# Between two stages of a hybrid decoder layer: the order of the second half's first products, and of a norm's sums

## Chip, cores and metric

The kernel runs on one core of a Trainium2 chip. The metric is the device time of the whole program in microseconds (us), the median of three runs.

## What is computed

One decoder layer on 512 tokens of width 1024, in float32: a gated feed-forward sub-layer, a mixing sub-layer (attention beside a state-space model), and a second feed-forward sub-layer. A norm stands before and behind each of them. Cut to what matters here:

```python
def rms_norm(x, g):
    y = x * lax.rsqrt(jnp.mean(x * x, axis=-1, keepdims=True) + NORM_EPS)
    return y * g

h = rms_norm(x, ffn1_pre_g)
x = x + 0.5 * rms_norm(swiglu(h, ffn1_w_in, ffn1_w_out), ffn1_post_g)
h = rms_norm(x, mix_pre_g)
proj = h @ w_mix_in                 # q, k, v, u
...                                 # attention and state-space model
x = x + rms_norm(mixed, mix_post_g)
h = rms_norm(x, ffn2_pre_g)
x = x + 0.5 * rms_norm(swiglu(h, ffn2_w_in, ffn2_w_out), ffn2_post_g)
```

The place of the change is between two sub-layers: from the last products of one, through its post-norm, the residual sum and the next pre-norm, to the first products of the next.

## The kernel before

Activations lie transposed: 8 k-tiles (`KD`) of 128 channels by 512 tokens. Each float32 product is made of three (`mm3`): an operand is rounded to a high part (`whi`, `xh`), the rest is its low part (`wlo`, `xl`), and high x high, high x low and low x high are added up in one PSUM bank. The high part is a cast on ScalarE (L93 for weights, L143 for activations), the low part a subtract on VectorE or GpSimd (L95, L144).

`boundary` stands between two stages and is called twice: between the first feed-forward stage and the mixing stage, and between that and the second feed-forward stage. Tokens are taken there in two halves of 256 (`h` 0 and 1). In order:

- The last products of the old stage (`product`, tile `yt`), first half and then second half, their sums into `y` (`gather`, L286) and the squares of `y` (`squares`).
- For each half the post-norm (`post[h]`): `sums` adds the squares over the channels with tiny products against ones (tile `st`), VectorE scales the result (`nv`, L182), GpSimd raises it to the power -1/2 (L184); `spread` copies the result to all partitions with four products (tile `rp`).
- `prep(h, k)` makes k-tile k of the next stage's input: VectorE scales `y` (L301), adds it to the residual `x` (L303), ScalarE makes `xh`, VectorE `xl`; ScalarE squares the new `x` and GpSimd adds the square to the next norm's sum (`sq_acc`, L155).
- `begin(h, k)` multiplies k-tile k with four chunks of the next stage's weights (`w`), three products each, into four banks (`first`). It is done on `x` before its norm; the norm's factor is applied to the results later.
- `pre[0]` is the next pre-norm's factor for the first half, `pre[1]` for the second; `pre[1]` is handed on and done inside the next stage.

In the second half, k-tiles 0 to 3 are multiplied k-tile by k-tile. Then come the sums of `pre[0]`, and then chunk by chunk: chunk 0 with k-tiles 4 to 7, chunk 1 with k-tiles 4 to 7, the spreading of `pre[0]`, and chunks 2 and 3. The post-norm of the second half, `post[1]`, is done inside the first half's products: its sums behind k-tile 3, its spreading behind k-tile 5.

The next stage begins with its own weight chunks (`prj` in the mixing stage, `gu` in the feed-forward stage). Rounded weights have four buffers for the high part and four for the low part (`wtiles`), and the four chunks of `boundary` fill all of them; raw weights have three.

Matmuls keep the order in which they are written. Most instructions of the other engines are put in order by the compiler's planner, which goes by its own estimate of what is ready; an instruction marked `fix` is pinned behind the one that was written just before it on its engine.

Of the kernel before, what the change touches and what calls it, by code (L numbers as in the profile page):

```python
# [20 lines left out]
KD = D // P  # L21
# [19 lines left out]
class Layer:  # L41
# [70 lines left out]
    def fix(self, i):  # L112
        return self.tc.keep_in_program_order(i)
# [143 lines left out]
    def boundary(self, y, tail, ipost, half, inext, chunks):  # L257


        nc = self.nc  # L260
        w = [self.load(c, (KD, P), pool=i % 2 == 1) for i, c in enumerate(chunks)]
        tw = [t.rearrange("p (m k j) -> p m k j", k=NT, j=P) for t in self.tw]
        hs = [slice(0, HT), slice(HT, S)]
        xh, xl = self.ktiles("xh", F32R), self.ktiles("xl", F32R)
        acc2 = self.acct()
        n4, nr = self.rtiles()
        o = [self.bank("first") for _ in w]
        p4 = self.sp.tile([P, 4], F32, name="p4", tag="p4")
        bank, acc = [None], [self.acct(), self.acct()]
        post = [self.rstd(acc[h], p4, None, 2 * h, 2 * h + 2, True) for h in range(2)]  # L270
        rr = [None, None]
        pre = [self.rstd(acc2, n4, nr, 0, 2), self.rstd(acc2, n4, nr, 2, 4)]

        def product(h, m):
            if m % 2 == 0 or m == 7:
                bank[0] = self.bank("yt").rearrange("p (m t) -> p m t", m=2)
            b = bank[0][:, m % 2 if m < 6 else 0]
            for k in range(NT):
                th, tl = tail(k)
                self.mm3(b, tw[0][:, m, k], tw[1][:, m, k], th[:, hs[h]], tl[:, hs[h]], k == 0, k == NT - 1)  # L280
            return bank[0]

        def gather(h, m, n, b, fix=lambda i: i):

            ym = y.pair(slice(m, m + n))[:, :, hs[h]]
            fix(nc.vector.tensor_tensor(out=ym, in0=b[:, :n], in1=ym, op=ALU.add))  # L286

        def squares(h, m, n, eng, fix=lambda i: i):

            m2 = slice(m % 2, m % 2 + n)  # L290
            t = (acc[h] if m == 0 else self.tmp("sq")).rearrange("p (m t) -> p m t", m=2)[:, m2]
            fix(nc.scalar.activation(out=t, in_=y.pair(slice(m, m + n))[:, :, hs[h]], func=AF.Square))
            if m and eng:
                ac = acc[h].rearrange("p (m t) -> p m t", m=2)[:, m2]
                (fix if eng is V else fx)(eng.tensor_tensor(out=ac, in0=ac, in1=t, op=ALU.add))
            return t.rearrange("p m t -> p (m t)")

        def prep(h, k, fix=lambda i: i):
            t = y(k)[:, hs[h]]
            xk = self.x(k)[:, hs[h]]  # L300
            fix(nc.vector.scalar_tensor_tensor(out=t, in0=t, scalar=self.g(ipost, k, half), in1=rr[h],  # L301
                                               op0=ALU.mult, op1=ALU.mult))
            fix(nc.vector.tensor_tensor(out=xk, in0=t, in1=xk, op=ALU.add))  # L303
            self.split(xh(k)[:, hs[h]], xl(k)[:, hs[h]], xk, self.g(inext, k), fix)
            self.sq_acc(acc2[:, hs[h]], xk, k == 0, nc.gpsimd)

        def begin(h, k, only=None):
            for i in range(len(w)) if only is None else (only,):
                self.mm3(o[i][:, hs[h]], w[i][0][:, k], w[i][1][:, k], xh(k)[:, hs[h]], xl(k)[:, hs[h]],
                         k == 0, k == KD - 1)  # L310

        V, G, fx = nc.vector, nc.gpsimd, self.fix
        b2 = [self.bank("yt")[:, :HT] for _ in range(2)]
        for ks in (range(NT - 1), (NT - 1,)):
            for m in range(2):
                for k in ks:
                    th, tl = tail(k)
                    self.mm3(b2[m], tw[0][:, m, k], tw[1][:, m, k], th[:, hs[0]], tl[:, hs[0]], k == 0, k == NT - 1)
        for m in range(2):
            gather(0, m, 1, b2[m].unsqueeze(1))  # L320
        squares(0, 0, 2, V)
        for m in range(2, KD):
            b = product(0, m)
            if m % 2 or m > 5:
                m, n = (m - 1, 2) if m < 6 else (m, 1)
                gather(0, m, n, b)
                squares(0, m, n, G if m == 2 else V)
        late = []
        for m in range(KD):
            b = product(1, m)  # L330
            if m % 2 or m > 5:
                m1, n = (m - 1, 2) if m < 6 else (m, 1)
                gather(1, m1, n, b)
                t = squares(1, m1, n, G if n == 2 else None)
                if n == 1:
                    late.append(t)
                if m == 5:
                    self.fold(acc[1], G, fx)
            if m == 2:
                post[0][0](fixp=fx)  # L340
            if m == 3:
                rr[0] = post[0][1]()
                for k in range(2):
                    prep(0, k)
        for k in range(KD):
            if k > 1:
                prep(0, k, fx if k > 5 else lambda i: i)
            begin(0, k)
            if k == 3:
                post[1][0](late, fix=fx)  # L350
            if k == 5:
                rr[1] = post[1][1]()
        for k in range(4):
            prep(1, k)
            begin(1, k)
        pre[0][0](fixp=fx)
        for k in range(4, KD):
            prep(1, k)
        for i in range(len(w)):
            for k in range(4, KD):  # L360
                begin(1, k, i)
            if i == 1:
                pre[0][1]()
        self.xh, self.xl = xh, xl
        return o, n4, nr, pre[1]
# [827 lines left out]
```

## Time and profile before

| | us |
|---|---|
| three runs | 978.39, 980.96, 981.84 |
| median | 980.96 |
| profiled execution, its own time | 978.9 |
| its span | 977.1 |

The profile is one execution, and its times count from the start of its span. PE is TensorE's matmul, PEld its weight load, DVE VectorE, ACT ScalarE, POOL GpSimd. A row of the timeline gives the start, the duration, the engine, the line, the operation, what it writes and reads, and how many instructions were merged; in brackets stands how long the engine was idle just before, and what it waited for. Most of TensorE's instructions have L121, a helper's line, so they are told apart by their tiles. `ymix` is `y` in the second call.

### The profile page before, as it was taken

The page shows a single profiled execution, that of the slowest core. Times are in us where ns is not written, and L with a number is a line of the kernel's source. Part 1 is how long each engine was busy: PE and PEld are TensorE (multiplying, and loading weights), DVE is VectorE, ACT ScalarE, POOL GpSimd, SP SyncE. Part 2 cuts the span into 40 slices and gives each one's busy share as a digit, 9 for nine tenths or more (in the row PEclk, how much of TensorE's full clock was granted, in tenths as well). Part 3 has the DMA queues.
Part 4 walks back from the last instruction along what each step waited for, and adds up shares of the span by engine and source line. Part 5 has one row for each costly group of instructions (what it writes and reads, how often), then busy time and mean ns, then how long its engine had stood idle before and what let it go on. Part 6 is the DMA issues. An engine that isn't in the chain of part 4 may idle for free.

```text
span 977.1 us, 12902 instructions
## 1 busy us (share of the span) xinstructions
PE 948.4 (97%) x5088; PEld 792.6 (81%) x5088; DVE 532.9 (55%) x938; ACT 372.3 (38%) x616; POOL 223.5 (23%) x134
## 2 busy tenths in 40 slices
PE   9999999999999999999999699999999999999996
PEld 7888888888888899878667589888888888888884
DVE  7997214553265447658769567564225433444426
ACT  7353334431233234356553654443333222323312
POOL 2322212322233134300000024422122212222300
PEclk9999999999999999999999999999999999999998
DMA  8223334343343230473111530222223222333202
GB/s 261 91 103 113 103 119 150 100 166 103 108 131 116 76 130 23 118 211 120 54 51 50 185 126 23 92 95 93 89 87 108 101 93 87 108 98 131 95 0 87
DMA packets 38606, 102.48 MB, mean 105 GB/s; under 512 B 7665, under 2 KB 10737, under 8 KB 38001
## 3 DMA queue, kind: packets, MB, share of 16 engines
q1 hardware_dynamic: 37680, 98.50, 31.6%
q10 hardware_dynamic: 864, 3.15, 0.9%
q8 instruction: 40, 0.66, 0.3%
q14 instruction: 22, 0.17, 0.1%
HBM read 94.03 MB, written 7.60 MB: 104 GB/s over the span
## 4 chain that ended last, share of the span: by engine, by line
PE 86%; DVE 7%; ACT 3%; DMA 2%; issue 1%; POOL 0%; DVEq 0%; POOLq 0%; ACTq 0%
PE gu L121 46%; PE yo L121 20%; PE prj L121 6%; PE yt L121 5%; PE first L121 4%; PE st L121 1%; DVE sx L1064 1%; DVE Hs L1064 1%; DVE xl L144 1%; DMA wraw<-wmot 1%; DVE x L303 1%; PE pt L820 1%; ACT sc L795 1%; DMA w<-w2d 1%; PE idle L121 1%
## 5 line engine op out<-in xcount | busy, mean ns | idle before, releaser
L93 ACT CAST whi<-wraw 128x1024 fp32r<-128x1024 f32 (+5 forms) x161 | 155.8, 971 | 323.8 <-PE gu L121 126.9
L95 POOL TENSOR_TENSOR wlo<-wraw,whi 128x1024 fp32r<-128x1024 f32 (+2 forms) x62 | 156.3, 2521 | 525.9 <-ACT whi L93 525.9
L121 PE MATMUL gu<-xh,whi 128*128 128x512 f32 x656 | 257.6, 393 | 0.0
L121 PE MATMUL gu<-xh,wlo 128*128 128x512 f32 x656 | 255.6, 390 | 0.0
L121 PE MATMUL gu<-xl,whi 128*128 128x512 f32 x656 | 255.3, 389 | 0.0
L95 DVE TENSOR_TENSOR wlo<-wraw,whi 128x1024 fp32r<-128x1024 f32 (+5 forms) x99 | 111.6, 1130 | 124.9 <-ACT whi L93 124.5
L121 PEld LDWEIGHTS gu<-xh,wlo 128*128 128x128 f32 x656 | 123.1, 188 | 25.9
L121 PEld LDWEIGHTS gu<-xl,whi 128*128 128x128 f32 x656 | 123.2, 188 | 25.1
L121 PEld LDWEIGHTS gu<-xh,whi 128*128 128x128 f32 x656 | 123.2, 188 | 25.1 <-issue 0.4
L405 DVE TENSOR_TENSOR ut<-gu,rs 128x512 f32<-128x512 f32 x41 | 28.3, 689 | 104.0 <-PE gu L121 103.8
L141 DVE TENSOR_TENSOR al<-ut,ah 128x512 fp32r<-128x512 f32 x44 | 69.0, 1570 | 24.9 <-ACT ah L140 24.8
L121 PE MATMUL yo<-ah,whi 128*128 128x512 f32 x144 | 56.0, 389 | 0.0
L121 PE MATMUL yo<-al,whi 128*128 128x512 f32 x144 | 56.0, 389 | 0.0
L121 PE MATMUL yo<-ah,wlo 128*128 128x512 f32 x144 | 56.0, 389 | 0.0
L121 PE MATMUL yo<-whi,ah 128*128 128x512 f32 x144 | 56.0, 389 | 0.0
L121 PE MATMUL yo<-wlo,ah 128*128 128x512 f32 x144 | 56.0, 389 | 0.0
L121 PE MATMUL yo<-whi,al 128*128 128x512 f32 x144 | 56.0, 389 | 0.0
L403 DVE TENSOR_TENSOR gt<-gu,rs 128x512 f32<-128x512 f32 x41 | 28.2, 688 | 50.7 <-PE gu L121 50.6
L140 ACT CAST ah<-ut 128x512 fp32r<-128x512 f32 x44 | 27.2, 621 | 58.3 <-DVE ut L406 58.2
L121 PE MATMUL first<-xl,whi 128*128 128x256 f32 (+1 forms) x144 | 43.3, 300 | 2.2 <-DVE xl L144 2.2
L121 PE MATMUL first<-xh,whi 128*128 128x256 f32 (+1 forms) x144 | 43.9, 305 | 0.9 <-ACT xh L143 0.9
L406 DVE TENSOR_TENSOR ut<-ut,gt 128x512 f32<-128x512 f32 x44 | 40.7, 927 | 3.7
(192 smaller groups left out, 1426.9 us busy)
## 6 DMA issues: line engine op xcount, KB each, us to landing
wraw<-w2i SPq DMA_DIRECT2D x44, 512.0 KB, 3.5
wraw<-w1i SPq DMA_DIRECT2D x42, 512.0 KB, 3.5
wraw<-w2o SPq DMA_DIRECT2D x18, 512.0 KB, 3.5
wraw<-wmi SPq DMA_DIRECT2D x16, 512.0 KB, 3.5
wraw<-w1o SPq DMA_DIRECT2D x16, 448.0 KB, 3.4
x<-xT SPq DMA_DIRECT2D x8, 256.0 KB, 4.5
w1d<-w1s SPq DMA_DIRECT2D x8, 256.0 KB, 2.9
w2d<-zb SPq DMA_DIRECT2D x2, 1024.0 KB, 4.9
```

The source lines that it names most:

```text
L93: fix(self.nc.scalar.copy(out=hi, in_=raw))
L95: fix(eng.tensor_tensor(out=lo, in0=raw, in1=hi.bitcast(F32), op=ALU.subtract))
L121: i = self.nc.tensor.matmul(*a, **k)
L140: nc.scalar.copy(out=hi, in_=src)
L141: nc.vector.tensor_tensor(out=lo, in0=src, in1=hi.bitcast(F32), op=ALU.subtract)
L144: fix(nc.vector.scalar_tensor_tensor(out=lo, in0=src, scalar=scale, in1=hi.bitcast(F32), op0=ALU.mult, op1=ALU.subtract))
L303: fix(nc.vector.tensor_tensor(out=xk, in0=t, in1=xk, op=ALU.add))
L403: nc.vector.tensor_tensor(out=gt, in0=o[f][0], in1=r, op=ALU.mult)
L405: nc.vector.tensor_tensor(out=ut, in0=o[f][1], in1=r, op=ALU.mult)
L406: nc.vector.tensor_tensor(out=ut, in0=ut, in1=gt, op=ALU.mult)
L795: nc.scalar.activation(out=so, in_=so, func=AF.Exp, bias=nm[:, t:t + 1], scale=-1.0, accum_out=den[:, t:t + 1])
L1064: tt = lambda o, x, y, op: self.fix(V.tensor_tensor(out=o, in0=x, in1=y, op=op))
```

## The change

The second half's products go k-tile by k-tile to the end; the sums of `pre[0]` stay behind k-tile 3, and its spreading stands behind k-tile 6. The sums of `post[1]` stand behind the first half's k-tile 2 instead of 3, and its spreading behind k-tile 4 instead of 5.

```diff
-        def begin(h, k, only=None):
-            for i in range(len(w)) if only is None else (only,):
+        def begin(h, k):
+            for i in range(len(w)):
                 self.mm3(o[i][:, hs[h]], w[i][0][:, k], w[i][1][:, k], xh(k)[:, hs[h]], xl(k)[:, hs[h]],
                          k == 0, k == KD - 1)
...
             if k > 1:
                 prep(0, k, fx if k > 5 else lambda i: i)
             begin(0, k)
-            if k == 3:
+            if k == 2:
                 post[1][0](late, fix=fx)
-            if k == 5:
+            if k == 4:
                 rr[1] = post[1][1]()
-        for k in range(4):
+        for k in range(KD):
             prep(1, k)
             begin(1, k)
-        pre[0][0](fixp=fx)
-        for k in range(4, KD):
-            prep(1, k)
-        for i in range(len(w)):
-            for k in range(4, KD):
-                begin(1, k, i)
-            if i == 1:
+            if k == 3:
+                pre[0][0](fixp=fx)
+            if k == 6:
                 pre[0][1]()
```

## Rows read from the trace of the kernel before

**Rows 1.** The page's part 4: the chain that ended last, by engine.

```profile
PE 86%; DVE 7%; ACT 3%; DMA 2%; issue 1%; POOL 0%; DVEq 0%; POOLq 0%; ACTq 0%
```

**Rows 2.** The chain in order of time, 605 to 626: start, us, what.

```profile
619.21 0.99 DVE xl L144
...
622.18 0.44 PE rp L121 x4
```

**Rows 3.** The timeline of TensorE in the second call, 603 to 640.

```profile
603.13 1.03 PE L121 MATMUL st<-ones,sq 128*128 128x2 f32 x8
...
606.98 0.60 PE L121 MATMUL rp<-ident,p 128*128 128x128 f32 x4
...
610.18 0.28 PE L121 MATMUL first<-xh,wlo 128*128 128x256 f32 x1
610.30 0.28 PE L121 MATMUL first<-xh,whi 128*128 128x256 f32 x1
610.90 0.38 PE L121 MATMUL first<-xl,whi 128*128 128x256 f32 x1 [0.32 <-DVE xl L144]
...
616.63 0.50 PE L121 MATMUL st<-ones,acc 128*128 128x2 f32 x4
...
620.24 0.38 PE L121 MATMUL first<-xl,whi 128*128 128x256 f32 x1 [0.63 <-DVE xl L144]
...
621.78 0.28 PE L121 MATMUL first<-xl,whi 128*128 128x256 f32 x1
...
625.34 0.40 PE L121 MATMUL gu<-xh,whi 128*128 128x512 f32 x1
...
626.04 0.40 PE L121 MATMUL gu<-xh,whi 128*128 128x512 f32 x1
...
633.30 0.61 PE L121 MATMUL rp<-ident,r 128*128 128x128 f32 x4
```

**Rows 4.** The timeline of VectorE, second call, 603 to 627.

```profile
603.26 0.42 DVE L303 TENSOR_TENSOR x<-ymix,x 128x256 f32<-128x256 f32 x1
...
605.51 0.15 DVE L182 TENSOR_SCALAR nv<-st 128x2 f32<-128x2 f32 x1
606.17 0.48 DVE L144 SCALAR_TENSOR_TENSOR xl<-x,sm,xh 128x256 fp32r<-128x256 f32 x1 [0.51 <-ACT xh L143]
607.62 0.87 DVE L301 SCALAR_TENSOR_TENSOR ymix<-ymix,sm,rp 128x256 f32<-128x256 f32 x2 [0.96 <-PE rp L121]
608.41 1.65 DVE L303 TENSOR_TENSOR x<-ymix,x 128x256 f32<-128x256 f32 x2
...
610.37 0.47 DVE L144 SCALAR_TENSOR_TENSOR xl<-x,sm,xh 128x256 fp32r<-128x256 f32 x1
...
621.75 1.74 DVE L95 TENSOR_TENSOR wlo<-wraw,whi 128x1024 fp32r<-128x1024 f32 x1 [1.56 <-ACT whi L93]
```

**Rows 5.** The timeline of GpSimd, second call, 603 to 640.

```profile
605.75 0.71 POOL L184 TENSOR_TENSOR p<-nv,mhalf 128x2 f32<-128x2 f32 x1 [3.59 <-DVE nv L182]
606.42 3.35 POOL L155 TENSOR_TENSOR acc<-acc,sq 128x256 f32<-128x256 f32 x4
...
619.18 3.23 POOL L155 TENSOR_TENSOR acc<-acc,sq 128x256 f32<-128x256 f32 x4
...
628.07 2.38 POOL L95 TENSOR_TENSOR wlo<-wraw,whi 128x1024 fp32r<-128x1024 f32 x1 [2.31 <-ACT whi L93]
```

**Rows 6.** The timeline of ScalarE, second call, 603 to 640.

```profile
620.66 1.05 ACT L93 CAST whi<-wraw 128x1024 fp32r<-128x1024 f32 x1 [1.18 <-PE first L121]
622.10 1.05 ACT L93 CAST whi<-wraw 128x1024 fp32r<-128x1024 f32 x1 [0.38 <-PE first L121]
...
626.94 1.05 ACT L93 CAST whi<-wraw 128x1024 fp32r<-128x1024 f32 x1 [1.91 <-DMA wraw<-w2i]
```

**Rows 7.** All instructions that write `wlo`: ns min/median/max, first and last start.

```profile
L95 DVE TENSOR_TENSOR wlo<-wraw,whi x99: 284/1224/2584, 6.8 to 919.6; 128x1024 fp32r<-128x1024 f32 x72, 128x512 fp32r<-128x512 f32 x12, 128x896 fp32r<-128x896 f32 x8, 128x256 fp32r<-128x256 f32 x4
```

**Rows 8.** The timeline of TensorE in the first call, 388 to 407.

```profile
390.33 0.28 PE L121 MATMUL first<-xh,whi 128*128 128x256 f32 x1
...
405.38 0.40 PE L121 MATMUL prj<-xh,whi 128*128 128x512 f32 x1
...
406.08 0.40 PE L121 MATMUL prj<-xh,whi 128*128 128x512 f32 x1
```

## The prediction, made before the changed kernel was run

> **What bounds the kernel now.** I read the page first, for the chain that ended last: TensorE carries 86% of it [rows 1]. Time is won only where TensorE waits, or where something that TensorE waits for comes earlier. Then I read the timeline of TensorE through the two calls of `boundary`. Both look alike: the first product of the second token half starts at 390.33 in the first call and at 610.30 in the second, and the next stage's first product starts 15.05 and 15.04 us later [rows 3, 8]. I work with the second call and carry the result to the first.
>
> In the second half TensorE starts a product every 0.12 us (610.18, 610.30) [rows 3]. Its 96 products would take 11.52 us. The next norm's sums (616.63) and their spreading interrupt them once each; the chain gives 0.44 us for the spreading [rows 2], and I take the same for the sums. So the half needs 12.40 us and takes 15.04: **2.64 us are waits**, with the slower restart after each. There are four waits. The first is at k-tile 0 (0.32 us idle at 610.90, VectorE's `xl` late), the last at k-tile 7 (0.63 us at 620.24, again `xl`) [rows 3]. The chain of waits between them runs through VectorE: its `xl` of k-tile 7 starts at 619.21 and takes 0.99 [rows 2]. The reader is to see why it is wanted so early: after k-tile 3 the kernel takes weight chunk 0 through k-tiles 4 to 7 at once, so k-tile 7 is wanted nine products (1.1 us) after k-tile 4, while VectorE makes k-tiles at the pace of one in some 1.3 us (`xl` of k-tile 0 ends at 610.84, of k-tile 7 at 620.20).
>
> Last I read ScalarE, for what the chunk order buys today. The next stage's weights are rounded into buffers that the four chunks hold. The cast at 622.10 starts 0.04 us after the last product that reads the high part of chunk 1 (starts 621.78, takes 0.28) [rows 3, 6]. The chunk-by-chunk end frees the first chunk early, and the rounding of the next weights hides under the other three.
>
> **The change, part by part.** No instruction is added or removed; the same products and sums are issued in another order, and no transfer is issued among the moved steps.
>
> *K-tile by k-tile to the end.* The second half's k-tile k is then wanted at 610.30 + 1.44k, plus 0.44 behind the sums and 0.44 more behind the spreading. For k-tile 7 that is 621.26; its `xl` ends at 620.20 today. All of the waits at k-tiles 4 to 7 go, without VectorE being a moment faster. What remains of the 2.64 us is the wait at k-tile 0: 0.60 us between two products instead of 0.12, and a restart 0.10 longer, 0.58 in all.
>
> *Sums and spreading of the second half's post-norm one k-tile earlier.* On TensorE the twelve tiny sum products end at 604.16 today (603.13 and 1.03) and the spreading starts at 606.98 [rows 3]; both move up by 1.44, and the first half's products fill the place, so TensorE's own work is unchanged. VectorE starts the second half's scaling at 607.62, released by the spreading [rows 4]. Moved by 1.44 it would be 606.18; `xl` of the first half's last k-tile stands there until 606.65 [rows 4], so I take 0.97 us earlier. K-tile 0's `xl` (ends 610.84) then ends near 609.9, and TensorE wants it at 610.42. The last wait goes too, and TensorE finishes the second half at 610.30 + 12.40 = 622.70.
>
> *The wait that the change brings.* All four chunks are now read up to k-tile 7. Chunk 0's high part is last read by the second of that tile's twelve products, 1.32 us before the end: it starts at 621.38, ends at 621.66, and the cast starts at 621.70. The cast takes 1.05 [rows 6] and VectorE starts the low part 0.04 later (621.75 today, after a cast that began at 620.66). That subtract took 1.74 there, beside GpSimd's adds; the median of the 99 is 1.224 [rows 4, 7]. GpSimd's four adds there end at 622.41 today (619.18 and 3.23 [rows 5]), and what they wait for comes earlier, so I take 1.224: it runs 622.79 to 624.01. TensorE restarts 0.06 later (as 610.84 to 610.90): the third product of the next stage, the first that reads the low part, starts at 624.07, and the fourth, after a slow restart, at 624.40. Unhindered the fourth would be at 622.70 + 0.70 = 623.40. So **1.00 us of new wait**; with the 1.74 us subtract it would be 1.5. Today the fourth product starts at 626.04: the gain is 1.64. In the first call the same sum gives 404.43 against 406.08, a gain of 1.65 [rows 8]. Queued behind the first cast on ScalarE are the casts for the next two chunks, at most 2.1 us and some 2.5 us of subtract more; they are wanted 24 products of 0.23 us (5.5 us) and 11 us later, and those products hide them.
>
> *The power behind the sums.* VectorE takes the sums at 605.51, 1.35 us after they ended, since the compiler's planner had put it behind the work of k-tile 7; GpSimd's power follows at 605.75 for 0.71 us and ends at 606.46, 0.52 before the spreading [rows 4, 5]. The new spreading stands at 605.54, so VectorE must take the sums by 604.59 or TensorE waits. Moved by a whole k-tile it would take them at 604.07, in the gap between `x` of k-tile 6 (ends 603.68) and its `xl`: no wait. In today's slot it would cost 0.92. The planner's order for VectorE is not fixed here and no row shows it, so the bounds are 0 and 0.92 per call; the first is nearer, because the sums also end a whole k-tile earlier for the planner. I take 0.15.
>
> *GpSimd's adds.* The power now stands ahead of five adds instead of four (today four in 3.35 us from 606.42, 0.84 each); the five end near 609. VectorE's `x` beside them took 1.65 for two, against 0.42 for one at 603.26 with GpSimd idle, so an operation that meets the adds loses 0.4 us on average [rows 4, 5]. Two more of VectorE's operations now fall beside them, `x` and `xl` of the first half's k-tile 7. They lose nothing if they miss the adds; 0.8 us by that row; and 1.68 if each waits out a whole add. The first two leave k-tile 0's `xl` at 609.87 to 610.67, a wait of 0 to 0.25 against 610.42. I take 0: the operations stand 0.5 us and more apart, so the first can fall before the adds. The third is rival D.
> The Trainium skill, SBUF — State Buffer, section "Who interferes with whom", says that a VectorE instruction with two SBUF inputs and a GpSimd instruction that reads SBUF exclude each other, and the later one waits for the whole of the other. By that rule the whole gain would be that of rival D, 0.5 us, where the sum by the row stays at 2.9. The trace shows the wait, at about half that price: 1.65 us for a pair whose own work is 0.84.
>
> *The later power in the last feed-forward stage.* The cast at 626.94 waits for a transfer [rows 6], which can start when the first subtract frees its buffer: 624.01 instead of 623.49. So GpSimd's subtract at 628.07 (2.38) [rows 5] moves to 628.6 and ends at 631.0; the second half's power behind it ends at 631.7. The spreading at 633.30 [rows 3] moves to 631.66. Bounds 0 (the power is put first) and 0.1; I take 0.1.
>
> **Sum**: 1.64 + 1.65 - 2 x 0.15 - 0.1 = 2.9 us. The profiled execution took 978.9 us (span 977.1), 2 us below the median of 980.96 and inside the three runs' spread. The forecast is 980.96 - 2.9 = **978.1 us**. I call a difference of under 0.3%, 2.9 us, no change; the forecast lies on that line. Between the calls nothing is tied to a fixed time: the mixing stage's work follows from TensorE's products and their results, so a gain at the first call should last.
>
> **Rivals.**
> *A. The forecast*, 977.0 to 979.2, chance 0.5.
> *B. The cover is not needed*: the next stage's weights are ready in time and only the waits vanish, 2 x 2.64 = 5.3, 975.7 us. For it: the raw weights lie there already. Against it: the casts of today wait for TensorE to let the buffers go. Chance 0.07.
> *C. The spreading comes before its power*: the sums are taken in today's slot, 0.92 us per call, of which 0.15 is in the forecast: 979.6 us. Chance 0.17.
> *D. The adds eat the advance.* Each of the two operations named above waits out an add: the scaling starts 1.68 us after 606.65, at 608.33, 0.71 later than today, and k-tile 0's `xl` ends at 611.55. TensorE waits 1.13 us and restarts 0.10 slower: of each call's 1.5 us some 0.25 is left, 980.4 us in all. For it: the adds run without a gap today. Against it: the row's 0.4 per operation. Chance 0.12. The rule of the page named above is this mechanism.
> *E. Slower*: VectorE takes the sums only behind `xl` of the first half's last k-tile (606.65). Then 0.15 for it, 0.09 to the power and 0.71: the spreading starts at 607.8 instead of 605.54, TensorE stands 2.26 us in each call, and no other wait is left. Per call 2.26 - 1.64 = 0.6 lost, 982.2 us. It turns the change into a loss from a wait of 1.64 us. For it: today VectorE is 1.35 late. Against it: no instruction waits for the sums' result but this one. Chance 0.08. Another 0.06 is for an unfixed order that shifts elsewhere, either way.
>
> **Numbers.** The line of 0.3% (978.0) cuts A in half. The three runs lie within 3.5 us, so a median may stand 1 us off, which carries a little of C and D over either line. Faster: 0.25 of A, 0.07 of B, 0.04 of the last case and 0.06 of C and D: 0.42. Slower by over 0.3% (above 983.9) needs E with more on top, or the last case: 0.08. Same: 0.50. The range runs from B, 975.6, to just past the median, 981.0, and leaves out E and part of the last case; A's own range is 977.0 to 979.2.
>
> **What would show it.** Right: no wait inside the second half's products but at the sums and the spreading; its span 12.4 us; then a wait of TensorE for ScalarE's cast and VectorE's subtract of about 1 us before the third product of `prj` and of `gu`; the scaling near 606.6 where it is 607.62. Wrong: a wait of TensorE at the spreading (C, E), at k-tile 0 (D), none at the stage's start (B), or a gain at the first call that is gone by the second.

## The result, and the profile after

| | median, us | runs |
|---|---|---|
| kernel before, beside it | 981.48 | 978.39 to 982.17 |
| changed kernel | 975.41 | 973.87 to 978.21 |

The ratio is 0.9943, with a 95% interval of 0.9928 to 0.9958: 5.6 us faster, 4.1 to 7.1. The forecast was 978.1 with a range of 975.6 to 981.0, so the median lies 0.2 us below the range. The profiled execution took 975.41 us, its span is 973.6. The page's chain that ended last, by engine, has two per cent of the span more on TensorE and two less on VectorE than in [rows 1]:

```profile
PE 88%; DVE 5%; ACT 3%; DMA 2%; issue 1%; POOL 0%; SPq 0%; DVEq 0%; POOLq 0%; ACTq 0%
```

The second call, TensorE, answers to [rows 3]. The call's first product starts at 595.38 here and at 597.00 before, so 1.62 us is taken off a time of before to compare it.

```profile
600.06 1.03 PE L121 MATMUL st<-ones,sq 128*128 128x2 f32 x8
...
603.91 0.60 PE L121 MATMUL rp<-ident,p 128*128 128x128 f32 x4
...
608.67 0.28 PE L121 MATMUL first<-xh,whi 128*128 128x256 f32 x1
...
621.21 0.50 PE L121 MATMUL gu<-xh,whi 128*128 128x512 f32 x1
621.54 0.40 PE L121 MATMUL gu<-xl,whi 128*128 128x512 f32 x1
622.47 0.50 PE L121 MATMUL gu<-xh,wlo 128*128 128x512 f32 x1 [0.53 <-DVE wlo L95]
622.80 0.39 PE L121 MATMUL gu<-xh,whi 128*128 128x512 f32 x1
```

No product of the second half (608.67 to 621.21) has a bracket any more: 12.54 us where it took 15.04. The one wait stands where the next stage begins, before its third product.

The chain in order of time shows what that wait is made of (compare [rows 2]): TensorE alone up to 619.81, then the cast, the subtract, and TensorE again.

```profile
605.00 9.60 PE first L121 x80
614.60 0.34 PE st L121 x4
614.94 4.42 PE first L121 x36
619.35 0.46 PE rp L121 x4
...
620.10 1.06 ACT whi L93
621.16 0.02 issue
621.18 1.24 DVE wlo L95
622.42 0.04 issue
622.47 3.70 PE gu L121 x15
```

VectorE and GpSimd in the same call answer to [rows 4, 5]: the sums are taken, then raised to their power, before the spreading wants them.

```profile
601.41 0.15 DVE L182 TENSOR_SCALAR nv<-st 128x2 f32<-128x2 f32 x1
...
602.99 0.46 DVE L303 TENSOR_TENSOR x<-ymix,x 128x256 f32<-128x256 f32 x1
604.02 0.48 DVE L144 SCALAR_TENSOR_TENSOR xl<-x,sm,xh 128x256 fp32r<-128x256 f32 x1 [0.58 <-ACT xh L143]
604.55 0.87 DVE L301 SCALAR_TENSOR_TENSOR ymix<-ymix,sm,rp 128x256 f32<-128x256 f32 x2
605.34 1.74 DVE L303 TENSOR_TENSOR x<-ymix,x 128x256 f32<-128x256 f32 x2
...
607.40 0.47 DVE L144 SCALAR_TENSOR_TENSOR xl<-x,sm,xh 128x256 fp32r<-128x256 f32 x1
```

```profile
601.65 0.71 POOL L184 TENSOR_TENSOR p<-nv,mhalf 128x2 f32<-128x2 f32 x1 [2.37 <-DVE nv L182]
602.33 4.47 POOL L155 TENSOR_TENSOR acc<-acc,sq 128x256 f32<-128x256 f32 x5
...
627.08 0.71 POOL L184 TENSOR_TENSOR r<-nv,mhalf 128x2 f32<-128x2 f32 x1 [2.42 <-DVE nv L182]
627.76 2.41 POOL L95 TENSOR_TENSOR wlo<-wraw,whi 128x1024 fp32r<-128x1024 f32 x1
```

The fourth product of the next stage starts 27.42 us after the call's first product (622.80 less 595.38), where it was 29.04 [rows 3]: 1.62 us won. The first call, TensorE, answers to [rows 8]; its first product starts at 377.51, and at 377.04 before:

```profile
404.60 0.50 PE L121 MATMUL prj<-xh,wlo 128*128 128x512 f32 x1 [0.53 <-DVE wlo L95]
404.94 0.39 PE L121 MATMUL prj<-xh,whi 128*128 128x512 f32 x1
```

The same wait, and the same difference goes from 29.04 to 27.43: 1.61. Both calls together are 3.2 us. Behind the second call all is as long as before: from the first `st` product behind `gu` to the end of TensorE's last product 338.19 us before and 338.20 after. The measured 5.6 us have another part, and what is left for it is the mixing stage between the two calls, where no line of code was changed. These two profiles alone do not show it: their spans differ by 3.5 us, and the mixing stage by 0.5. Why is told under "Where the rest of the gain comes from".

### The profile page after: what moved, and what is told of

Same layout as the page of the kernel before. It is cut to its first block, busy times and chain, and to the rows that moved or that the text cites. A ratio compares the mean times of both kernels' runs of the same rounds, so it can differ in the third digit from the quotient of the medians.

```text
span 973.6 us, 12902 instructions
## 1 busy us (share of the span) xinstructions
PE 949.2 (97%) x5088; PEld 791.1 (81%) x5088; DVE 531.0 (55%) x938; ACT 372.7 (38%) x616; POOL 222.5 (23%) x134
## 4 chain that ended last, share of the span: by engine, by line
PE 88%; DVE 5%; ACT 3%; DMA 2%; issue 1%; POOL 0%; SPq 0%; DVEq 0%; POOLq 0%; ACTq 0%
PE gu L121 46%; PE yo L121 20%; PE prj L121 6%; PE first L121 5%; PE yt L121 5%; PE st L121 1%; DVE Hs L1060 1%; DVE sx L1060 1%; PE pv L121 1%; PE pt L816 1%; ACT sc L791 1%; ACT whi L93 1%; DMA w<-w2d 1%; DMA wraw<-wgl 1%; DVE so L141 1%
## 5 line engine op out<-in xcount | busy, mean ns | idle before, releaser
L121 PE MATMUL first<-xh,wlo 128*128 128x256 f32 (+1 forms) x144 | 42.4, 295 | 0.0
```

The source lines that it names most:

```text
L121: i = self.nc.tensor.matmul(*a, **k)
```

## The experiments

Three stretches are compared in every profile, each from the start of one product to the start of another. *Call 1*: from the first `first` product of the first call to the first `st` product in the mixing stage. *Call 2*: the same for the second call. *Mixing*: from the end of the one to the start of the other. Inside it, *ys to yt* runs from the first `ys` product to the first `yt`. The last column is how long after its issue the first `wmot` transfer is taken up by ScalarE's cast (`wmot` are the weights of the mixing stage's output tail; `pv` are products of its attention, `ys` of its state-space model, `yt` its last ones). The ratio is to the kernel before, timed beside it.

| kernel | ratio, 95% | call 1 | call 2 | mixing | ys to yt | wmot |
|---|---|---|---|---|---|---|
| before | | 31.09 | 32.45 | 188.87 | 43.46 | 4.87 |
| before again | 1.0003, 0.9989 to 1.0018 | 31.13 | 32.46 | 191.41 | 43.50 | 4.96 |
| changed | 0.9943, 0.9928 to 0.9958 | 29.50 | 30.85 | 188.37 | 40.04 | 3.61 |
| changed, second | 0.9920, 0.9901 to 0.9939 | 29.48 | 30.85 | 186.89 | 40.58 | 3.88 |
| changed, third | 0.9943, 0.9927 to 0.9958 | 29.48 | 30.84 | 189.11 | 41.05 | 3.52 |
| post-norm moved alone | 0.9997, 0.9979 to 1.0016 | 29.10 | 30.46 | 194.44 | 43.18 | 4.42 |
| k-tile by k-tile alone | 0.9952, 0.9934 to 0.9969 | 30.13 | 31.46 | 190.38 | 43.37 | 4.65 |
| last two k-tiles by chunk | 0.9935, 0.9917 to 0.9953 | 28.80 | 29.80 | 191.18 | 43.30 | 4.82 |
| first call alone | 0.9956, 0.9943 to 0.9970 | 29.51 | 32.09 | 191.77 | 43.81 | 4.94 |
| second call alone | 0.9982, 0.9968 to 0.9995 | 31.11 | 30.87 | 190.43 | 43.49 | 4.96 |
| changed, call 2 by chunk | 0.9929, 0.9911 to 0.9946 | 29.51 | 29.80 | 186.75 | 40.20 | 3.58 |

### The parts of the change

*The post-norm's sums and spreading moved, the second half as before.*

```diff
-            if k == 3:
+            if k == 2:
                 post[1][0](late, fix=fx)
-            if k == 5:
+            if k == 4:
                 rr[1] = post[1][1]()
```

> One part alone: the second half's post-norm one k-tile earlier, the chunk-by-chunk end kept. Theory (by the timeline): the wait at k-tile 0 goes, 0.58 us; VectorE then runs some 1 us ahead, but k-tile 7 is still wanted 1.1 us after k-tile 4, so of the three later waits (2.06 us with their restarts) about 1 us is left; the next stage's weights stay hidden. Gain about 1.6 us a call, 3.2 us in all. Rival (the moved post-norm is worth only the wait it removes): 0.6 us a call, 1.2 us in all.

The calls gave 1.99 us each, where 1.6 was expected, and more than the change as a whole: with the chunk order kept there is no wait at the next stage's start, and the scalings' earlier start ends most of the waits (the second half takes 13.06 us in call 2). The expected 3.2 us did not come, because the mixing stage became longer. From the end of call 1 to the second group of `pv` products it took 78.15 us, and 72.16 to 72.23 in every other profile of the study: the planner had put the conversions there in another order, and TensorE waits for two of them (before had no such wait between 412 and 440) and restarts at a lower clock (0.82 from 425 to 430):

```profile
425.85 0.50 PE L121 MATMUL prj<-xh,whi 128*128 128x512 f32 x1 [2.19 <-ACT whi L93]
428.17 0.79 PE L121 MATMUL prj<-xh,wlo 128*128 128x512 f32 x1 [1.58 <-DVE wlo L95]
```

So a change inside the calls can be eaten by the order of unpinned instructions outside them.

*K-tile by k-tile alone*: the changed kernel with `k == 3` and `k == 5` put back for the post-norm.

> The other part alone: the second half k-tile by k-tile to the end, the post-norm where it was. Theory: the wait at k-tile 0 stays (0.58 us) and at most 0.2 us more at k-tiles 1 and 4; the waits at k-tiles 5 to 7 go (2.06 us); TensorE stands 1.0 us before the third product of the next stage. Gain 1.0 us a call, 2 us in all. Rival (the gain of the whole change is larger than its waits, because something outside the two calls got faster): more than 3.5 us in all, with the two calls' own stretches shorter by 1 us each only.

The calls gave 0.96 and 0.99, as expected. In call 2 the wait at k-tile 0 is still there, and so is the one at the stage's start:

```profile
611.94 0.39 PE L121 MATMUL first<-xl,whi 128*128 128x256 f32 x1 [0.34 <-DVE xl L144]
...
625.71 0.50 PE L121 MATMUL gu<-xh,wlo 128*128 128x512 f32 x1 [0.53 <-DVE wlo L95]
```

The time fell by 4.7 us (3.0 to 6.5), more than the calls' 2.0, as the rival had it; its profile was the slowest of its six executions.

*The new wait taken away*: the changed kernel, but the last two k-tiles chunk by chunk.

```diff
         for k in range(KD):
             prep(1, k)
-            begin(1, k)
+            if k < KD - 2:
+                begin(1, k)
             if k == 3:
                 pre[0][0](fixp=fx)
-            if k == 6:
-                pre[0][1]()
+        for i in range(len(w)):
+            for k in range(KD - 2, KD):
+                begin(1, k, i)
+            if i == 0:
+                pre[0][1]()
```

> The changed kernel, but k-tiles 6 and 7 chunk by chunk, with the spreading behind chunk 0. Theory: chunk 0 is free about 1.1 us sooner, so the wait before the third product of the next stage goes from 1.0 us to under 0.1; k-tile 7 is wanted 1.1 us sooner and is still there in time. 0.9 us a call, 1.8 us in all faster than the changed kernel, about 7 us faster than before. Rival (the cover is not what is missing: the wait moves to k-tile 7's xl, or to the cast behind the copy of the factor): within 0.5 us of the changed kernel.

The calls gave 2.29 and 2.65 us, 0.7 and 1.05 more than the change. TensorE at the start of the feed-forward stage runs through:

```profile
622.60 0.40 PE L121 MATMUL gu<-xh,whi 128*128 128x512 f32 x1
622.83 0.40 PE L121 MATMUL gu<-xl,whi 128*128 128x512 f32 x1
623.07 0.39 PE L121 MATMUL gu<-xh,wlo 128*128 128x512 f32 x1
```

So the wait for the first chunk's release is the price of the k-tile order, and letting that chunk go earlier buys it back: whole in call 2, and in call 1 all but 0.3 us. The planner returned to the mixing order of before, and the expected gain of 1.8 us over the changed kernel is not seen in the time: the ratios are 0.9935 and, for the changed kernel beside it, 0.9920.

*The changed kernel a second time.*

> The changed kernel once more, unaltered, beside the others. Theory: the two calls' stretches show 1.6 us each again, and the whole 3.2 to 3.6 us below before; the first timing's 5.6 us held some 2 us of scatter from the mixing stage. Rival: 5 to 6 us again, with a share that comes from outside the two calls in every run.

The calls repeat to 0.02 us. The time is 7.9 us under before (6.0 to 9.7), so the theory of 3.2 to 3.6 us fell: a share from outside the calls is there again, as the rival said.

### Where the rest of the gain comes from

Before the second call the changed kernel differs from the kernel before in one more thing than the first call: VectorE and ScalarE convert two of the mixing stage's weight chunks earlier, and SyncE issues two `wmi` transfers ahead of the `ud` stores instead of behind them. (K-tile by k-tile alone and the last two k-tiles by chunk have the mixing order of before, but for one cast of ScalarE.) To part this from the calls, the change was made at one call only (`moved` picks the old or the new code; `ipost` is 1 in the first call and 3 in the second):

```diff
+        moved = ipost == 1
```

> The change at the first call (ffn1 to mixing) alone; the second call as before. Engine orders before the second call are those of the changed kernel, the mixing stage's among them. Theory: the first call's stretch (first product of `first` to first product `st`) is 29.5 us against 31.1, the second's stays at 32.45, and the mixing stage keeps what its other order of conversions gives: the stretch from the first `ys` to the first `yt` is 40 to 40.6 us where before it was 43.5. Time 1.6 + about 2.4 = 4 us under before. Rival (the rest of the gain is scatter of the mixing stage that comes with any order): that stretch lies anywhere between 40 and 43.5, and the time is 1.6 us under before.

> The change at the second call (mixing to ffn2) alone; every engine's order up to that call is that of before, the mixing stage's among them. Theory: the first call's stretch stays 31.1 us, the second's is 30.85 against 32.45, the stretch from the first `ys` to the first `yt` stays 43.3 to 43.5 us, time 1.6 us under before. Rival: the same calls, but that stretch may be 40 to 43.5 us as well, and time 1.6 us under before, give or take 1.5.

> The kernel before, unchanged, timed against itself: ratio 1.000 within 0.002. Theory (the mixing stage's order, not chance, sets the stretch from the first `ys` to the first `yt`): 43.3 to 43.5 us again. Rival (chance): anywhere from 40 to 43.5. The calls' stretches 31.1 and 32.45 us by either.

> The changed kernel, but in the second call the last two k-tiles of the second half run chunk by chunk, with the spreading behind the first chunk, so that the next stage's first weight buffer comes free some 4 us earlier; the first call and the mixing stage's order stay those of the changed kernel. Theory: the wait of 1 us before the next stage's third product goes, the second call's stretch is 29.8 us against the changed kernel's 30.85, the first's 29.5, the stretch from the first `ys` to the first `yt` 40 to 40.6; time 1 us under the changed kernel's, 6.6 to 8 us under before. Rival (the earlier loads collide with the last scalings, or the wait moves to the fourth product): 30.85 and no gain over the changed kernel.

By time the first theory holds, and before again shows 43.50 us from `ys` to `yt`, as expected. The second call alone gives 1.8 us (0.5 to 3.1) for 1.6 in its stretch, the first alone 4.3 (2.9 to 5.6) for 1.6 in its own. They add up to 6.1, within the change's interval. (In the profile of the first call alone the second call is 0.36 us shorter too, 32.09 for an expected 32.45: its wait at k-tile 0 is gone.) By profile the theory's stronger form falls: the first call alone has the changed kernel's order up to the second call, and its profiled execution took 43.81 us from `ys` to `yt`. Its executions lie between 973.37 and 979.65 us, and the profiled one was the longest. The last of the four shows the wait of 1 us gone from call 2 (29.80 us), and a time (7.0 us under before, 5.3 to 8.7) that can't be told from the changed kernel's. The first cast came 1.55 us earlier in that call, not some 4.

What makes this stretch long or short is seen on the queue of SyncE and on TensorE. Before:

```profile
535.36 0.33 SPq L99 DMA_DIRECT2D wraw<-wmot  x1
535.78 0.53 SPq L910 DMA_DIRECT2D w<-w2d  x1
...
542.56 0.33 SPq L99 DMA_DIRECT2D wraw<-wmot  x1
544.07 0.53 SPq L910 DMA_DIRECT2D w<-w2d  x1
```

```profile
541.85 0.64 PE L121 MATMUL ys<-Hs,w 128*32 128x128 f32 x16 [3.07 <-DMA w<-w2d]
...
550.33 1.08 PE L121 MATMUL ys<-Hs,w 128*32 128x128 f32 x16 [2.57 <-DMA w<-w2d]
```

After:

```profile
536.85 0.33 SPq L99 DMA_DIRECT2D wraw<-wmot  x1
537.27 0.53 SPq L906 DMA_DIRECT2D w<-w2d  x1
...
542.79 0.33 SPq L99 DMA_DIRECT2D wraw<-wmot  x1
545.19 0.53 SPq L906 DMA_DIRECT2D w<-w2d  x1
```

```profile
543.20 0.64 PE L121 MATMUL ys<-Hs,w 128*32 128x128 f32 x16 [2.87 <-DMA w<-w2d]
...
550.06 0.64 PE L121 MATMUL ys<-Hs,w 128*32 128x128 f32 x16 [0.95 <-DMA w<-w2d]
```

A 512 KB `wmot` transfer and a `w2d` transfer are issued 0.42 us apart. Where `wmot` is taken up after 3.5 to 3.9 us, its buffer comes free early, the next `wmot` starts 2.4 us or more ahead of the next `w2d`, and that `w2d` makes TensorE wait 0.95 to 1.10 us (not at all in the third profile of the changed kernel). Where it takes 4.4 to 5.0 us, the lead is 1.5 us and the wait 2.57 to 3.18. Behind the long wait TensorE restarts at its lower clock (1.08 us for the same 16 products that take 0.64). These windows show it. A row gives the window, its length, and the busy time and number of instructions of TensorE's matmuls and weight loads, VectorE, ScalarE and GpSimd. The third column from the end is TensorE's granted clock, a mean over the window (1.00 is the higher of its two levels, 2.4 GHz, and 0.50 the lower, 1.2); behind it stand the DMA share and GB/s. Before:

```profile
480.00:485.00 5.00, 4.71 (x32) 3.25 (x33) 1.64 (x6) 4.32 (x10) 0.88 (x1) 1.00 0.00 0
...
550.00:555.00 5.00, 4.67 (x91) 4.15 (x92) 1.59 (x2) 2.04 (x3) 0.00 (x0) 0.66 0.23 91
```

After:

```profile
480.00:485.00 5.00, 5.00 (x28) 3.15 (x25) 2.43 (x7) 4.01 (x9) 0.00 (x0) 0.67 0.16 52
...
550.00:555.00 5.00, 4.59 (x96) 3.76 (x97) 3.16 (x4) 3.93 (x6) 0.00 (x0) 1.00 0.63 220
```

Before again, the same program as before:

```profile
480.00:485.00 5.00, 4.16 (x19) 2.04 (x20) 1.64 (x5) 3.60 (x9) 1.04 (x1) 0.67 0.00 0
```

Six profiles with the transfers' long form have an order other than the changed kernel's, four with the short form have the changed kernel's, and one long one (the first call alone) has it too. So the order does not fix the form, it goes with its odds. The clock's fall at 480 is luck of the execution: the same program has 1.00 there in one profile and 0.67 in another, behind the same wait of 2.00 us. It costs 1.6 us (from the second `pv` group to the third 26.31 us or 27.95). A second place is like it: from 505 to 510 the granted clock is 1.00 before and 0.72 after, and the stretch from the third `pv` group to the first `ys` takes 20.35 us or 21.39. The profile that the prediction was made from had neither fall, the changed kernel's had both; this hides most of the gain in the mixing stage when these two are compared. Among profiles with both falls the stage took 191.41 us (before again) and 188.37 and 189.11 (changed): 2.3 to 3.0 us less.

The mean granted clock of the timed executions is on record, so the time lost to the lower clock can be estimated for each, as (1 - clock) x span. It was 8.7 us on average in 75 executions of the kernel before and 5.8 in 15 of the changed kernel. Among the 75, one microsecond more of it went with 0.8 us more time, so the 2.9 us between the two averages stand for some 2.3 us, about what the calls leave unexplained in two of the three timings of the changed kernel (2.4; the other leaves 4.7). This is an estimate and shows what the rest goes with, not its cause: the lower clock behind the long wait is a part of the long form.

### The place with the luck taken away

The raw tail weights (`wmot`) get a buffer of their own, so that no `w2d` transfer queues behind one that waits for its buffer:

```diff
-            raw, hi, lo = self.wtiles(shape[0] * shape[1], into)
+            if own is None:
+                raw, hi, lo = self.wtiles(shape[0] * shape[1], into)
+            else:
+                raw, (hi, lo) = own.tile([P, 1024], F32, name="traw", tag="traw", bufs=1), into
...
-        tail = lambda c: self.load_tail(a["wmot"], c, False)
+        tail = lambda c: self.load_tail(a["wmot"], c, False, bdm)
```

> The kernel before, but the raw weights of the mixing stage's output tail (`wmot`) get a buffer of their own, so that the `w2d` transfers, which TensorE waits for in the `ys` products, are issued ahead of them. Theory of the place (these waits and the clock's fall behind them make the stretch from the first `ys` to the first `yt` 43.5 us, and in lucky executions 40): waits for `w` of 5.6 us fall under 1.5, no fall of the clock there, the stretch is 38 to 40 us, time 4 to 5 us under before. Rival (the tail weights are late in their place): the wait moves to the `gl` or `yt` products and the time stays within 1.5 us of before.

> The changed kernel with the same buffer. With the `ys` waits gone in both, the difference to the run just before it is the change without that place's luck. Theory: 3.2 us (1.6 per call, the two calls' stretches 29.5 and 30.85 us), with under 1 us from the mixing stage. Rival (the other order of conversions that the changed kernel has in the mixing stage is itself worth 2 to 4 us, wherever the ys waits are): 5 to 7 us.

> The kernel whose second halves run the last two k-tiles chunk by chunk (both calls, call stretches 28.8 and 29.8 us), with the same buffer. Theory: gains add up: 1.8 us under the changed kernel with the buffer, 4.9 us under before with the buffer, so 9 to 10 us under before. Rival (mixing stage's order of before costs what the changed order gains): no better than the changed kernel with the buffer.

> The changed kernel unchanged, a third profile. Theory (chance sets which of two lengths the stretch from the first `ys` to the first `yt` has): 40 or 43.5 us, with the calls at 29.5 and 30.85; times spread over 972 to 979 us. Rival (its order fixes the short one): 40 to 40.6 us again, and no time above 977. Ratio to before 0.992 to 0.995 by either.

| with the buffer | median, us | ratio to before, 95% | ys to yt |
|---|---|---|---|
| before | 979.21 | 0.9977, 0.9966 to 0.9989 | 40.54 |
| changed | 975.51 | 0.9941, 0.9923 to 0.9958 | 40.86 |
| last two k-tiles by chunk | 972.69 | 0.9912, 0.9895 to 0.9928 | 41.09 |
| (changed, without the buffer) | 975.31 | 0.9943, 0.9927 to 0.9958 | 41.05 |

The waits at `ys` are gone in all three kernels with the buffer, and the kernel before gained 2.3 us, half of what was expected: as the rival said, waits behind them grow, at `gl` from 0.87 to 2.23 us and at `yt` from 0.72 to 1.60 (kernel before with the buffer):

```profile
558.49 0.50 PE L124 MATMUL gl<-zz,whi 128*128 128x512 f32 x1 [2.23 <-ACT zz L143]
...
575.35 1.82 PE L124 MATMUL yt<-so,tw 128*128 128x256 f32 x13 [1.60 <-DVE so L144]
```

What counts here is the difference between the first two rows: 0.9977 less 0.9941 is 3.5 us, near the 3.2 of the two calls. With both intervals it is 1.5 to 5.6, so the rival's 5 us is not quite excluded. (The calls took 32.52 and 32.11, 29.48 and 30.85, 28.78 and 29.80 us in the three profiles; 32.52 has a fall of the clock in it.) The changed kernel gains nothing from the buffer (0.9941 and 0.9943). The expectation that its time spreads over both forms was half met: the third profile has the short form once more, the times run from 974.29 to 978.55. The last kernel has the lowest time of this table, 8.6 us under before (7.1 to 10.3, expected 9 to 10) and 2.8 under the changed kernel with the buffer (expected 1.8).

## Why the prediction was right in the calls and short in all

**The waits of the second half: right.** All four went; 12.54 us against 12.40.

**The wait at the next stage's start: right, term by term.** From the call's first product the cast was forecast at 24.70 us and came at 24.72 (620.10); the subtract at 25.79 and 25.80, with 1.23 us for 1.224. The fourth product stands 0.89 us later than it would unhindered (622.80 for 621.21 + 0.70), forecast 1.00. The kernel with the last two k-tiles by chunk shows the cause: release the first chunk earlier and the wait is gone in call 2 (0.3 us are left in call 1). Rival B (cover not needed) gives 975.7 us, next to the measured time, and is wrong: its mechanism is not there. A time alone does not tell which rival won.

**The power behind the sums: a term of 0.15 per call that was not there.** VectorE took the sums 0.32 us after they ended (601.41; the eight products end at 601.09), and the power ended at 602.36, 1.55 us before the spreading. Rivals C and E fall. (E's own sum has a slip: 606.65 and its three terms make 607.60, not 607.8, so E stood for some 981.8 us.)

**GpSimd's adds: right to take 0.** Five adds now run from 602.33 to 606.80, and the scaling started 9.17 us after the call's first product instead of 10.62, the whole 1.44 earlier rather than 0.97: the first half's last `xl`, which was to hold it up, moved too and ends at 604.50, 0.53 earlier. TensorE does not wait at k-tile 0. The two operations that were to meet the adds took 0.46 us (602.99) and 0.48 (604.02). The pair of `x` behind them took 1.74 us, near the 1.65 of before [rows 4]. One by one, beside the adds:

```profile
605.34 0.86 DVE L303 TENSOR_TENSOR x<-ymix,x 128x256 f32<-128x256 f32 x1
605.18 0.74 POOL L155 TENSOR_TENSOR acc<-acc,sq 128x256 f32<-128x256 f32 x1
...
606.13 0.96 DVE L303 TENSOR_TENSOR x<-ymix,x 128x256 f32<-128x256 f32 x1
606.00 0.80 POOL L155 TENSOR_TENSOR acc<-acc,sq 128x256 f32<-128x256 f32 x1
```

Each `x` ended 0.28 or 0.29 us behind the add that was running when it started. So it waited for what was left of that add. It lost 0.44 and 0.54 us over the 0.42 of one alone, less than a whole add. The Trainium skill, SBUF — State Buffer, section "Who interferes with whom", states that a VectorE instruction with two SBUF inputs contends with a GpSimd instruction that reads SBUF, and that the contention is an exclusive lock; the trace agrees. To price that as a whole add for each operation was rival D's step, and D falls.

**The later power in the last feed-forward stage: 0.1 that was not there.** The planner put the power (627.08) before the subtract (627.76), the lower of the two bounds.

So the two calls give 3.2 us where 2.9 was forecast after the deductions. **The step that failed** is the sentence that the mixing stage follows from TensorE's products and that a gain at the first call should last, with only 0.06 for an order that shifts elsewhere. It lasts, but the stage between is not the same afterwards: the planner orders its conversions and transfers otherwise. What in the change makes it do so is not shown. It is not alone that the four weight buffers come free together, for in k-tile by k-tile alone they do so too and the order stays that of before. With the changed order the mixing stage was shorter on average (188.1 us in three profiles of the changed kernel, 190.2 in the two of before and that of the second call alone). With the post-norm moved alone a third order cost 6.0 us. It is this part that took the median below the forecast's range; the forecast for the calls was right for its reasons.

**What stays open.** Why the two transfers end in the short form mostly under the changed order was not found: instructions and queues are the same there, and the times of the first call alone spread as if it had both forms. K-tile by k-tile alone speaks against the order as the only cause: it has the mixing order of before and still gained 2.7 us more than its calls.

## What to carry to other kernels

After a local change, compare the order of the unpinned instructions behind it, not only the place itself. A planner that orders them by its own estimate can move conversions and transfers of a whole stage away: here the stage behind came out 2 us shorter on average in one case and 6 us longer in another, against 3.2 us won in the place itself.

Where an order by k-tile makes a supplier's pace harmless and an order by chunk frees buffers early, mix them: k-tile by k-tile to the last two, and chunk by chunk over those, kept both gains but for 0.3 us in call 1.

Judge a part by stretches between two marks of the profile, which repeated here to 0.04 us in the profiles of one program where its whole time scattered by 4 to 7, and time the unchanged kernel against itself.

## What the hardware showed beside it

A wait of a few microseconds can cost more than itself: behind one, 16 small products took 1.08 us instead of 0.64 at a granted clock of 0.66. It struck some executions of a program and not others, also in a call: the kernel before with the buffer had 0.66 from 400 to 405 us, behind the waits of 0.44 and 0.63 us that the kernel before has there too, and its first call took 32.52 us instead of 31.09.

```profile
400.00:405.00 5.00, 4.44 (x26) 4.44 (x27) 0.50 (x1) 0.65 (x2) 4.20 (x5) 0.66 0.60 210
```

Two 512 KB transfers issued 0.42 us apart ended in one of two ways, the first one taken up after 3.5 to 3.9 us or after 4.4 to 5.0, with nothing between in eleven profiles.
